# Batched 64x64 matrix products: b three tiles ahead instead of four, half of two a tiles as fp32, and casts and result blocks given to other engines

## The chip, the cores and the metric

The kernel runs on one core of a Trainium2 chip. The metric is the device time of one execution in microseconds (us), the median of several. A profile gives a span, which is about 1.8 us shorter than the time of the same execution. MB are millions of bytes, and a "tile" of b or of the result is 64 matrices (1 MiB as fp32), of a 128 matrices (2 MiB).

## The reference

```python
a: float32 (1024, 64, 64);  b: float32 (1024, 64, 64)
return np.matmul(a, b).astype(np.float32)      # float32 (1024, 64, 64)
```

So 33.55 MB are read and 16.78 MB are written, with little arithmetic for each byte.

## The kernel before

There are 8 tiles of a (index s) and 16 of b and of the result (index t). A tile of a comes in four quarters (h): three are cast to bf16 by the DMA itself, on GpSimd's queue, the fourth comes as fp32 and VectorE casts it (the very first tile comes wholly as fp32). TensorE transposes a, VectorE spreads it into a block-diagonal tile, casts b to bf16, and ScalarE (for odd tiles VectorE too) moves the products from PSUM to SBUF. b comes on SyncE's queue for even t and on ScalarE's for odd t; all results go out on GpSimd's queue.

```python
A_AHEAD = 3;  B_AHEAD = 4                       # buffers of a_pool and of b_pool
...
def load_a(s):
    a_sb = a_pool.tile([128, 3, 16, 64], bf16, name="a_sb")
    for h in range(3):
        nc.gpsimd.dma_start(out=a_sb[:, h, :, :]..., in_=a_v[s, h])
    a_raw = a_pool.tile([128, 16, 64], fp32, name="a_raw")
    nc.sync.dma_start(out=a_raw[:]..., in_=a_v[s, 3])
...
def load_b(t):
    b_sb = b_pool.tile([128, 16, 128], fp32, name="b_sb")
    queue = nc.scalar if t % 2 else nc.sync
    queue.dma_start(out=b_sb[:], in_=b_v[t])
...
for t in range(n_t):                            # s, half = t // 2, t % 2
    if t + 1 < n_t:
        spread(t + 1)
        cast(t + 1)
    if t + B_AHEAD < n_t:
        load_b(t + B_AHEAD)
    if half == 0 and 0 < s < n_s - 1 - A_AHEAD:
        load_a(s + 1 + A_AHEAD)
    if half == 0 and 0 < s < n_s - 1:
        transpose(s + 1, 1)
    multiply(t)
    ...                                         # regroup, transpose(s + 2, 0), store(t - 1)
```

## Time and profile before

| | before |
|---|---|
| time, median of 4 | 135.45 us (135.24 to 135.5) |
| span of the profile | 133.8 us |
| busiest engines | VectorE 71%, ScalarE 66% |
| HBM bytes per time, from 4 us to the last read | 399 GB/s |
| last packet of a read, of a store | 109.65, 131.9 us |

On each queue the packets follow the order of issue, so adding up their sizes tells when each transfer began and ended. A packet of a casting load counts twice, since it reads twice the bytes that it writes. "The end of the reads" below is always the end of the last packet of a or b. Packet times here are counted from the zero of the profile's views; those in the prediction lie 0.25 us later, which changes no difference between two of them, but makes a wait from an issue to a packet look 0.25 us longer.

These are the last stretches of the kernel before: start and end, length, then busy time of PE, PEld, DVE, ACT and POOL with the number of instructions, granted clock, DMA share and GB/s.

```profile
108.00:116.00 8.00, 5.22 (x105) 4.90 (x101) 7.24 (x10) 6.88 (x13) 2.25 (x2) 0.57 1.03 402
116.00:124.00 8.00, 2.04 (x64) 1.92 (x64) 4.72 (x11) 5.22 (x12) 4.52 (x6) 0.89 1.02 372
124.00:134.00 10.00, 0.00 (x0) 0.00 (x0) 0.00 (x0) 0.00 (x0) 0.00 (x0) 0.50 0.67 231
```

In the last 10 us no engine computes at all; the DMA share of 0.67 is that of the last stores. Whatever is computed a few microseconds later than here costs nothing, as long as the stores in front of it are still going out.

### The profile page before, as it was taken

Reading aid. Unit: us, or ns where it says so; the run is one execution under the profiler, and the core shown is the slowest. Engines: PE = TensorE matmul, PEld = TensorE weight load, DVE = VectorE, ACT = ScalarE, POOL = GpSimd, SP = SyncE. Lnnn points to the kernel's source line nnn. Section 1 sums busy time; section 2 is a strip of 40 time slices with the busy share of each in tenths; the row PEclk is TensorE's granted clock in tenths of the full one; section 3 lists DMA queues with packets and bytes.
Section 4 is the critical chain, followed back from the end, with each engine's and each line's share of the span. In section 5 each row is a group of like instructions: output and inputs, shape, how many; then the busy total and the mean of one; then the engine's idle time right before and its main releaser. Section 6 shows DMA issues by size and latency. Waiting matters only on the chain.

```text
span 133.8 us, 2832 instructions
## 1 busy us (share of the span) xinstructions
PE 65.7 (49%) x1152; PEld 62.7 (47%) x1152; DVE 94.6 (71%) x120; ACT 87.7 (66%) x161; POOL 38.5 (29%) x49
## 2 busy tenths in 40 slices
PE   0007307970077463749919744991876376640000
PEld 0007207970077353649909744991866266630000
DVE  5930499108997059999999999899959989992000
ACT  3225424998038996758998985899793987992000
POOL 8991000420091080334124042003301220637000
PEclk9999999999559999555996896589677775797555
DMA  3999999999999999999999999999999999999991
GB/s 75 376 331 311 306 315 311 307 301 309 306 307 382 366 312 309 388 397 397 317 304 352 399 392 377 314 307 364 398 385 391 392 401 398 404 388 353 338 334 42
DMA packets 17485, 45.01 MB, mean 336 GB/s; under 512 B 1088, under 2 KB 1088, under 8 KB 17472
## 3 DMA queue, kind: packets, MB, share of 16 engines
q0 software_dynamic: 7440, 22.28, 54.8%
q1 hardware_dynamic: 5520, 13.11, 27.0%
q10 hardware_dynamic: 4512, 9.44, 18.6%
q8 instruction: 9, 0.15, 0.4%
q14 instruction: 4, 0.03, 0.1%
HBM read 33.55 MB, written 16.78 MB: 376 GB/s over the span
## 4 chain that ended last, share of the span: by engine, by line
DMA 35%; SPq 27%; DVE 15%; issue 6%; ACT 3%; POOL 3%; PE 3%; POOLq 1%; DVEq 0%; ACTq 0%
SPq L72 22%; DMA a_raw<-in_a_dram 18%; DMA b_sb<-in_b_dram 17%; DVE at_bd L128 8%; DVE b_bf L139 5%; SPq L91 3%; POOL out_dram L161 3%; PE o_ps L184 3%; ACT o_sb L172 2%; DVE o_sb L172 1%; SPq L85 1%; ACT b_bf L146 1%; DVE a_bf L106 1%; DVE a_bf L103 1%; POOLq L278 1%
## 5 line engine op out<-in xcount | busy, mean ns | idle before, releaser
L172 ACT COPY o_sb<-o_ps 64x512 f32<-64x512 f32 x106 | 61.6, 581 | 14.3 <-PE o_ps L184 13.0
L184 PEld LDWEIGHTS <-at_bd 128*128 128x128 bf16 x1024 | 41.6, 111 | 34.9 <-DVE b_bf L139 22.4
L184 PE MATMUL o_ps<-b_bf,at_bd 128*128 128x64 bf16 x960 | 41.9, 215 | 31.1 <-DVE b_bf L139 20.9
L128 DVE COPY at_bd<-at_sb 32x1024 f32<-32x1024 f32 x64 | 46.0, 719 | 13.4 <-ACT at_sb L118 11.6
L161 POOL DMA_DIRECT2D out_dram<-o_sb x20 | 20.6, 1031 | 58.1 <-ACT o_sb L172 21.4
L115 PE MATMUL at_ps<-identity,a_bf 128*128 128x128 f32 x128 | 23.4, 360 | 20.6 <-ACT a_bf L100 11.0
L115 PEld LDWEIGHTS at_ps<-identity,a_bf 128*128 128x128 f32 x128 | 21.6, 196 | 20.8 <-issue 19.3
L118 ACT COPY at_sb<-at_ps 128x512 f32<-128x512 f32 x32 | 16.9, 596 | 8.2 <-PE at_ps L115 8.0
L68 POOL DMA_DIRECT2D a_sb<-in_a_dram x21 | 13.9, 673 | 25.9 <-DVE a_bf L103 19.9
L139 DVE CAST b_bf<-b_sb 128x2048 bf16<-128x2048 f32 x14 | 17.4, 1245 | 2.9 <-DMA b_sb<-in_b_dram 2.6
L172 DVE COPY o_sb<-o_ps 64x512 f32<-64x512 f32 x14 | 9.7, 690 | 0.6 <-ACT o_sb L172 0.3
L106 DVE CAST a_bf<-a_raw 128x1024 bf16<-128x1024 f32 x7 | 5.5, 792 | 5.7 <-DMA a_raw<-in_a_dram 5.7
L103 DVE COPY a_bf<-a_sb 128x3072 bf16<-128x3072 bf16 x7 | 7.0, 1006 | 0.0
L100 ACT CAST a_bf<-o_sb 128x1024 bf16<-128x1024 f32 x2 | 2.1, 1044 | 5.0 <-DMA o_sb<-in_a_dram 5.0
L139 ACT CAST b_bf<-b_sb 128x2048 bf16<-128x2048 f32 x1 | 1.9, 1898 | 3.8 <-DMA b_sb<-in_b_dram 3.8
L100 DVE CAST a_bf<-o_sb 128x1024 bf16<-128x1024 f32 x2 | 2.8, 1380 | 1.9 <-DMA o_sb<-in_a_dram 1.9
L212 DVE MEMSET at_bd<- 128x4096 f32 x1 | 3.5, 3472 | 0.8 <-issue 0.8
L172 DVE COPY o_sb<-at_ps 64x256 f32<-64x256 f32 x8 | 3.4, 422 | 0.3 <-PE at_ps L184 0.2
L172 ACT COPY o_sb<-at_ps 64x256 f32<-64x256 f32 x8 | 2.9, 367 | 0.1
L209 ACT ACT_TABLE_LOAD x1 | 1.3, 1283 | 2.3 <-issue 2.3
L184 PE MATMUL at_ps<-b_bf,at_bd 128*128 128x64 bf16 x64 | 2.0, 193 | 1.2 <-DVE at_bd L128 1.2
L217 POOL MEMSET at_bd<- 128x2048 f32 x1 | 1.8, 1849 | 0.0
(12 smaller groups left out, 5.5 us busy)
## 6 DMA issues: line engine op xcount, KB each, us to landing
out_dram<-o_sb POOLq DMA_DIRECT2D x14, 1024.0 KB, 23.6
a_sb<-in_a_dram POOLq DMA_DIRECT2D x21, 256.0 KB, 17.4
a_raw<-in_a_dram SPq DMA_DIRECT2D x7, 512.0 KB, 24.2
o_sb<-in_a_dram ACTq DMA_DIRECT2D x2, 512.0 KB, 7.0
o_sb<-in_a_dram SPq DMA_DIRECT2D x2, 512.0 KB, 5.9
out_dram<-o_sb POOLq DMA_DIRECT2D x2, 512.0 KB, 11.4
out_dram<-o_sb POOLq DMA_DIRECT2D x4, 256.0 KB, 10.1
b_sb<-in_b_dram SPq DMA_DIRECT2D x8, 0.5 KB, 22.2
```

What stands on the lines that cost most here:

```text
L68: nc.gpsimd.dma_start(out=a_sb[:, h, :, :].rearrange("p v k -> p (v k)"), in_=a_v[s, h])
L72: nc.sync.dma_start(out=a_raw[:].rearrange("p v k -> p (v k)"), in_=a_v[s, 3])
L100: copy(a_bf[:, :, h, :], a_sb[h].rearrange("p (v k) -> p v k", v=16))
L103: nc.vector.tensor_copy(a_bf[:, :, 0:3, :], cast_sb[:].rearrange("p h v k -> p v h k"))
L106: nc.vector.tensor_copy(a_bf[:, :, 3, :], raw[:])
L115: nc.tensor.transpose(at_ps[:, vo, :], a_cols[:, 4 * vo + 2 * j + wl, :], identity[:])
L118: nc.scalar.copy(at_tiles[s][:, j, :, wl, :, :], at_ps[:].rearrange("p vo (g mp) -> p g mp vo", mp=4),)
L128: nc.vector.tensor_copy(bd[rows, :, :, :, h, :].rearrange("p j g wl mo -> p j (g wl) mo"), at_tiles[t // 2][rows, :, half, :, :, :].rearrange(
L139: (nc.vector.tensor_copy if t else nc.scalar.copy)(b_bf[:], b_sb[:])
L161: nc.gpsimd.dma_start(out=o_v[t, :, lo : lo + n, :], in_=o_sb[:, lo : lo + n].rearrange("p gh j wl n -> p (gh j wl n)"),)
L172: copies[2 * par + wl](dst, src)
L184: nc.tensor.matmul(o_ps[:, gl, g % 2, j, :], at_bd[:, j, g, :, u], b_bf[:, g, 64 * u : 64 * u + 64], start=(u == 0), stop=(u == 1),)
```

## The change

The intent, as I read it: an earlier end of the tail. GpSimd's queue, which carries all results, gets two casting loads less; VectorE gives two casts of b to GpSimd; ScalarE gives result blocks to VectorE; and a b buffer is given up, which pays for the two new fp32 buffers.

```diff
-    B_AHEAD = 4
+    B_AHEAD = 3
+    x_pool = ctx.enter_context(tc.tile_pool(name="x_pool", bufs=2))
...
     def load_a(s):
+        n_cast = 3 if s < n_s - 2 else 2
         a_sb = a_pool.tile([128, 3, 16, 64], bf16, name="a_sb")
-        for h in range(3):
+        for h in range(n_cast):
             nc.gpsimd.dma_start(...)
-        a_raw = a_pool.tile([128, 16, 64], fp32, name="a_raw")
-        nc.sync.dma_start(..., in_=a_v[s, 3])
+        for h in range(n_cast, 4):
+            pool = a_pool if h == 3 else x_pool
+            raws[h] = pool.tile([128, 16, 64], fp32, name=f"a_raw{h}")
+            queue = nc.sync if h == 3 else nc.scalar
+            queue.dma_start(..., in_=a_v[s, h])
...                                             # regroup: one VectorE cast for each fp32 quarter
     def cast(t):
-            (nc.vector.tensor_copy if t else nc.scalar.copy)(b_bf[:], b_sb[:])
+                engine = nc.gpsimd if t >= n_t - 3 else nc.vector      # t = 0 stays on ScalarE
+                engine.tensor_copy(b_bf[:], b_sb[:])
...
-                if half and t % 2:
+                if half and (t % 2 or t >= n_t - 4):
                     copies[2:] = [nc.vector.tensor_copy] * 2
...
         transpose(0, 1)
-        load_b(3)
         spread(0)
```

More of the change, by code (lines that the diff above doesn't have):

```diff
@@ L70, in load_a @@
             )
-        a_raw = a_pool.tile([128, 16, 64], fp32, name="a_raw")
-        nc.sync.dma_start(out=a_raw[:].rearrange("p v k -> p (v k)"), in_=a_v[s, 3])
-        a_tiles[s] = a_sb, a_raw
+        raws = {}
+        for h in range(n_cast, 4):
+            pool = a_pool if h == 3 else x_pool
+            raws[h] = pool.tile([128, 16, 64], fp32, name=f"a_raw{h}")
+            queue = nc.sync if h == 3 else nc.scalar
+            queue.dma_start(out=raws[h][:].rearrange("p v k -> p (v k)"), in_=a_v[s, h])
+        a_tiles[s] = a_sb, raws
     def load_first_a():
@@ L101, in regroup @@
         else:
-            cast_sb, raw = a_sb
+            cast_sb, raws = a_sb
+            n_cast = 4 - len(raws)
             nc.vector.tensor_copy(
-                a_bf[:, :, 0:3, :], cast_sb[:].rearrange("p h v k -> p v h k")
-            )
-            nc.vector.tensor_copy(a_bf[:, :, 3, :], raw[:])
+                a_bf[:, :, 0:n_cast, :],
+                cast_sb[:, 0:n_cast].rearrange("p h v k -> p v h k"),
+            )
+            for h, raw in raws.items():
+                nc.vector.tensor_copy(a_bf[:, :, h, :], raw[:])
         abf_tiles[s] = a_bf
@@ L138, in cast @@
         if t < n_t - 1:
-            (nc.vector.tensor_copy if t else nc.scalar.copy)(b_bf[:], b_sb[:])
+            if t == 0:
+                nc.scalar.copy(b_bf[:], b_sb[:])
+            else:
+                engine = nc.gpsimd if t >= n_t - 3 else nc.vector
+                engine.tensor_copy(b_bf[:], b_sb[:])
         else:
```

## The prediction

> **What bounds the kernel now.** I read the slices of the page first, then its queues, then the waits of the SyncE queue, then the trace's packet records (start, size and queue of every DMA packet), which I added up per queue in stretches of 4 us.
>
> ```profile
> PE 65.7 (49%) x1152; PEld 62.7 (47%) x1152; DVE 94.6 (71%) x120; ACT 87.7 (66%) x161; POOL 38.5 (29%) x49
> ...
> DMA  3999999999999999999999999999999999999991
> GB/s 75 376 331 311 306 315 311 307 301 309 306 307 382 366 312 309 388 397 397 317 304 352 399 392 377 314 307 364 398 385 391 392 401 398 404 388 353 338 334 42
> ...
> q0 software_dynamic: 7440, 22.28, 54.8%
> q1 hardware_dynamic: 5520, 13.11, 27.0%
> q10 hardware_dynamic: 4512, 9.44, 18.6%
> ...
> HBM read 33.55 MB, written 16.78 MB: 376 GB/s over the span
> ```
>
> No compute engine is above 71%, while the DMA row is full from the second slice to the last but one. The GB/s row seems to dip to 310 wherever a tiles are fetched, but it counts what is written: a casting load of a reads 512 KB and writes 256 KB. Counted by HBM bytes (a cast packet twice), the packet records give 383 to 412 GB/s in every 4 us stretch from 4 to 120 us, 398 in the mean. Only the ends fall short: 0.36 MB in the first 4 us, and 353, 343 and 253 GB/s in the stretches from 120 to 132 us.
>
> ```profile
> SPq L278 <- DMA out_dram<-o_sb: 41.8, 3, 40.8
> ```
>
> ```profile
> 118.34 3.03 ACT L172 COPY o_sb<-at_ps 64x256 f32<-64x256 f32 x8
> 118.61 0.75 POOL L161 DMA_DIRECT2D out_dram<-o_sb  x1 [1.46 <-ACT o_sb L172]
> 120.14 2.96 POOL L161 DMA_DIRECT2D out_dram<-o_sb  x4 [0.77 <-ACT o_sb L172]
> ```
>
> These are the SyncE queue's final wait (for stores) and the end of the timeline. Computing is over at 121.4 us; the last store packet starts near 132 us. Stores go out in order on the GpSimd queue (q0), so its packets tell when each is served: tile 12's store is issued at 108.7 and begins at 118.9, tile 13's at 113.8 and 121.9, tile 14's at 116.2 and 124.9, tile 15's at 120.1 and 127.9. Every late store waits 8 to 10 us behind earlier ones. The kernel is **bound by DMA bytes**; the chain of waits, which names SyncE's a_raw issues and b loads, describes the order in which a full pipe serves them. Its weight there comes from this line of the a_raw tile:
>
> ```profile
> L72 SPq DMA_DIRECT2D a_raw<-in_a_dram x7: 550/11657/13702, 3.3 to 65.5; - x7
> ```
>
> A hardware-queue issue normally takes 0.7 us (b_sb: 707 ns); an a_raw issued right behind a b load holds its sequencer for 6 to 14 us, until roughly a tenth to a quarter of that b tile has moved.
>
> **What the Trainium skill says.** "DMA: Bandwidth & Descriptors", Queues, rings and completion order: each DMA engine goes round its queue rows packet by packet. The trace agrees: while all three queues have work, b moves at about 100 GB/s on q1 and 93 on q10 in 2 KB packets, stores at about 190 on q0 in 4 KB packets. Same page, Specifications: 358 GB/s of HBM per core and a fabric ceiling of 435; this case measures 398, between them, and I use 398. "GPSIMD Engine Reference", Performance versus the Vector engine: 1.03 cycles per element for the shortest loop bodies and 1.8 for the best longer one, at 1.2 GHz, so I estimate a 2048-element cast at 1.8 to 3.1 us. The trace has no GpSimd cast; its 2048-element memset took 1.85 us. "SBUF — State Buffer", SBUF: two separate sides: GpSimd and a VectorE operation in a two-port mode lock each other out for a whole instruction. No GpSimd compute meets VectorE late in this trace, so no run yet shows it.
>
> **The change part by part.**
>
> *b three ahead.* The same 16 loads; from tile 3 on each is allowed one tile later. The b casts are (110.38 - 51.70)/10 = 5.9 us apart (tiles 4 to 14). On ScalarE's queue b landed early: last packet to cast is 14.5, 9.8, 6.5, 6.4 and 8.0 us for tiles 5, 7, 9, 11, 13, so 5.9 us later mostly fits. On SyncE's queue b lands just in time (3 us or less from tile 8 on), but there it waits for the queue and not for its buffer: tile 12 is issued at 77.6 and starts at 88.8, tile 14 at 88.2 and 98.5. A 5.9 us later issue is absorbed. In the start-up, b tile 3 is issued after ScalarE's cast of tile 0 (ends 20.97) instead of at 14.77; its queue then idles from 19.65 to about 22.5 and the other two take the bandwidth. It also puts a_raw 3 ahead of b 4 on SyncE's queue, which should remove the 5.7 us for which VectorE waited for a_raw at 42.5; b 4 itself then lands near the time at which it was cast before (51.7), so I count no gain. **Sum 0.**
>
> *Half of the last two a tiles as fp32.* Two 512 KB reads move from q0 to q10. HBM bytes are unchanged (50.33 MB). Cast stretches run near 402 GB/s and cast-free ones near 394: 1.05 MB costs 0.05 us more. GpSimd saves two issues of 0.67 us; VectorE's 3072-element bf16 copy (0.955 us) becomes 2048 elements plus one more 1024-element cast (0.69), some 0.4 us more on each of two tiles, off the DMA path. The new load is issued from ScalarE right behind a b load, so the hold seen on SyncE can occur on an engine that computes: I estimate 1.5 to 4 us of held ScalarE at tiles 4 and 6, when the results of those tiles wait for it. **Sum +0.1 on the DMA, up to 8 us of ScalarE that the pipe should hide.**
>
> *GpSimd casts tiles 13 and 14.* VectorE loses 2 x 1.23 us, GpSimd gains 2 x (1.8 to 3.1) us and VectorE may be locked out for as long. The stores of tiles 11 and 12 stand behind these casts in GpSimd's order, so they are issued some 3 to 5 us later; they had 13 and 10 us to spare. **Sum 0.**
>
> *VectorE takes two result blocks from tile 12 on.* For tiles 12 and 14, two copies each: ScalarE loses 4 x 0.58 = 2.3 us, VectorE gains 4 x 0.69 = 2.8 us. The last computing may end a microsecond earlier, but tile 15's store waits 7.8 us for its turn anyway. **Sum 0.**
>
> So the sum is 135.4 + 0.05 to 0.1. The best case: the first 4 us as they are, the other 49.97 MB at 398 GB/s (125.6 us), 1.6 us from the last packet to the end of the span (132.2 to 133.8), and 1.65 us by which the time exceeds the span: 4 + 125.6 + 1.6 + 1.65 = 132.9 us, 1.9% down. **That is the ceiling of any gain**, and nothing in the change speaks to the slow last 12 us directly.
>
> **The rivals.** First, *ScalarE becomes a bound*: two holds of up to 4 us delay evacuation, hence PE, hence later stores. For it: ScalarE shows 9, so 90% or more, in many of the later slices, and holds of 12 us are there on SyncE. Against it: q10's previous b tile should be nearly through, and the late stores have 8 us to spare. If the holds are 10 us each, the backlog is used up and the time becomes 137 to 140. Second, *starvation*: with three b buffers the reads could end later and the stores be served sooner, so that the final backlog shrinks and the tail computing (b 15 landed to last store issued, some 10 us) comes into the open. For it: q10 will idle for some microseconds early on. Against it: loading and computing step every 5.9 us, while a tile's whole DMA (a, b and out, 3.15 MB) takes 7.9 us at 398 GB/s, so the stores fall behind by the difference. It would cost 1 to 4 us. Third, *a quicker tail*: if the slow last 12 us come from one queue writing alone, moving 1 MB off q0 shortens them; 3.8 MB at 340 rather than 398 costs 1.6 us in all, so a gain of 0.3 to 1 us, 134.5.
>
> **Range and chances.** The sum says 135.4, the third rival pulls down by up to 1, the other two up by more but with little weight. I predict **135.2 us, range 133.7 to 137.4**. Faster by over 2% needs less than 132.7, below the ceiling of 132.9: 0.03. Slower by over 2% needs the first two rivals to eat 8 us of backlog and 2.7 more: 0.07. Within 2%: 0.90.
>
> **What would show it.** Right: the DMA row full as before, the same 398 GB/s of HBM bytes in the middle, computing over 5 us or more before the last packet, the a_raw wait at 42 us gone, casts of 2 to 4 us on GpSimd. Wrong: a DMA slice under 9 in the middle or late, late stores served at once after issue, or a ScalarE issue of an fp32 a load lasting over 8 us. A rate above 400 GB/s would also break it.

## The result, and the profile after

The changed kernel takes 136.27 us (median of 4, 136.11 to 136.49) against 135.45: a ratio of 1.0064, 95% interval 1.0044 to 1.0085. Here and below a ratio is the mean time of one kernel's fast runs over the mean of the other's in the same rounds, so not quite the ratio of the medians. It is 0.6% slower: inside the stated range and "within 2%", but clear of noise, and on the other side of the stated centre.

The page of the changed kernel: slices and queues, to be held against those of before in the prediction.

```profile
DMA  3999999999999999999999999999999999999693
GB/s 78 365 331 310 307 314 278 277 308 328 328 324 392 304 327 347 389 394 388 317 349 393 403 389 335 326 396 386 395 394 393 392 394 394 390 381 350 232 319 110
...
q0 software_dynamic: 7152, 21.76, 52.5%
q1 hardware_dynamic: 5520, 13.11, 26.7%
q10 hardware_dynamic: 4800, 10.49, 20.4%
```

The bytes moved as told: 1.05 MB more on q10 (ScalarE), the 0.52 MB that two casting loads write off q0. The middle is nearly as full as before (397 GB/s of HBM bytes from 4 us to the last read, against 399). What is new is the 6 in the third slice from the end, with 232 GB/s: the DMA engines wait there. The stretches of the end say for what.

```profile
116.00:124.00 8.00, 6.29 (x128) 6.12 (x127) 5.14 (x8) 4.99 (x10) 3.90 (x4) 0.56 1.00 373
124.00:134.00 10.00, 0.11 (x4) 0.00 (x0) 4.76 (x10) 3.23 (x9) 3.78 (x6) 0.62 0.72 244
```

From 124 us on, VectorE still works for 4.8 us and ScalarE for 3.2, where both were done before. The issues of the last stores, from the timeline of the changed kernel:

```profile
117.02 0.89 POOL L175 DMA_DIRECT2D out_dram<-o_sb  x1
...
119.34 1.40 POOL L175 DMA_DIRECT2D out_dram<-o_sb  x1 [1.42 <-issue]
...
123.41 0.77 POOL L175 DMA_DIRECT2D out_dram<-o_sb  x1 [2.67 <-ACT o_sb L186]
...
126.27 2.94 POOL L175 DMA_DIRECT2D out_dram<-o_sb  x4 [2.10 <-ACT o_sb L186]
129.54 0.72 POOL L175 DMA_DIRECT2D out_dram<-o_sb  x1 [0.33 <-DVE o_sb L186]
```

By the packet records tile 12's store starts at 119.1, tile 13's at 122.0, tile 14's at 125.1: 2.1, 2.7 and 1.7 us after their issue, where they stood in line for 10.0, 7.8 and 8.4 us before. At tile 14's second half the line is gone: it is issued at 126.27 and starts at 127.6, and from 126 to 128 us the DMA moves 221 and then 137 GB/s. Computing ends at 129.25 us (before: 121.4), the last packet at 132.9.

The reason is upstream: the reads end at 118.9 us, 9.3 us later than before. From there the chain is serial: b tile 15's casts at 119.58, its products from 121.28, its blocks copied out until 129.25. The total of the reads is the same, and nearly the rate; the stores were only served earlier and the reads later. The change's own blocks stand in this chain too: VectorE ends last, 1.9 us after ScalarE (127.4), because it first copies two blocks of tile 14 (1.39 us from 124.33).

ScalarE's holds are there too. These are its issues of the new fp32 loads:

```profile
52.20 5.15 ACTq L79 DMA_DIRECT2D a_raw<-in_a_dram  x1
...
66.89 4.68 ACTq L79 DMA_DIRECT2D a_raw<-in_a_dram  x1
```

So there were three suspects: reads that end late because fewer b loads are in flight (theory 1 below), the holds of ScalarE (theory 2, a part of theory A), and a tail in which GpSimd's casts or VectorE's blocks take longer (theories 3 and B).

### The profile page after: what moved, and what is told of

The parts are those of the page before. It is cut to its first block, busy times and chain, and to the rows that moved or that the text cites. A ratio compares the mean times of both kernels' runs of the same rounds, so it can differ in the third digit from the quotient of the medians.

```text
span 134.7 us, 2843 instructions
## 1 busy us (share of the span) xinstructions
PE 64.7 (48%) x1152; PEld 62.1 (46%) x1152; DVE 94.2 (70%) x124; ACT 85.5 (63%) x157; POOL 41.3 (31%) x49
## 4 chain that ended last, share of the span: by engine, by line
ACT 25%; DMA 23%; PE 18%; DVE 14%; issue 7%; ACTq 5%; POOL 2%; SPq 1%; POOLq 1%
DMA b_sb<-in_b_dram 23%; ACT o_sb L186 19%; PE o_ps L198 12%; DVE at_bd L138 7%; PE at_ps L125 6%; DVE o_sb L186 4%; ACT at_sb L128 4%; ACTq L79 4%; DVE b_bf L153 2%; POOL out_dram L175 2%; ACT b_bf L150 1%; ACTq L98 1%; SPq L92 1%; DVE a_bf L111 1%; POOLq L291 1%
## 5 line engine op out<-in xcount | busy, mean ns | idle before, releaser
L186 ACT COPY o_sb<-o_ps 64x512 f32<-64x512 f32 x102 | 59.3, 581 | 8.5 <-PE o_ps L198 7.1
L198 PEld LDWEIGHTS <-at_bd 128*128 128x128 bf16 x1024 | 43.2, 113 | 42.8 <-DVE b_bf L153 16.3
L125 PE MATMUL at_ps<-identity,a_bf 128*128 128x128 f32 x128 | 21.3, 337 | 19.1 <-ACT a_bf L107 11.4
L125 PEld LDWEIGHTS at_ps<-identity,a_bf 128*128 128x128 f32 x128 | 19.5, 181 | 19.1 <-issue 19.1
L153 DVE CAST b_bf<-b_sb 128x2048 bf16<-128x2048 f32 x12 | 15.1, 1260 | 8.2 <-DMA b_sb<-in_b_dram 8.0
L71 POOL DMA_DIRECT2D a_sb<-in_a_dram x19 | 12.2, 655 | 21.6 <-DVE a_bf L111 19.5
L186 DVE COPY o_sb<-o_ps 64x512 f32<-64x512 f32 x18 | 12.4, 690 | 8.9 <-ACT o_sb L186 8.6
L153 POOL CAST b_bf<-b_sb 128x2048 bf16<-128x2048 f32 x2 | 4.1, 2066 | 10.9 <-DMA b_sb<-in_b_dram 10.9
L111 DVE COPY a_bf<-a_sb 128x3072 bf16<-128x3072 bf16 (+1 forms) x7 | 6.1, 877 | 0.0
L160 ACT CAST b_bf<-b_sb 128x512 bf16<-128x512 f32 x2 | 1.1, 615 | 2.9 <-DMA b_sb<-in_b_dram 2.9
```

What stands on the lines that cost most here:

```text
L71: nc.gpsimd.dma_start(out=a_sb[:, h, :, :].rearrange("p v k -> p (v k)"), in_=a_v[s, h])
L111: nc.vector.tensor_copy(a_bf[:, :, 0:n_cast, :], cast_sb[:, 0:n_cast].rearrange("p h v k -> p v h k"),)
L125: nc.tensor.transpose(at_ps[:, vo, :], a_cols[:, 4 * vo + 2 * j + wl, :], identity[:])
L153: engine.tensor_copy(b_bf[:], b_sb[:])
L186: copies[2 * par + wl](dst, src)
L198: nc.tensor.matmul(o_ps[:, gl, g % 2, j, :], at_bd[:, j, g, :, u], b_bf[:, g, 64 * u : 64 * u + 64], start=(u == 0), stop=(u == 1),)
```

## The experiments

All twelve were timed in five rounds against the kernel before, and all gave correct results.

### Each part alone

**e1_b3**, three b buffers and tile 3's load moved, nothing else:

```diff
-    B_AHEAD = 4
+    B_AHEAD = 3
...
-        load_b(3)
```

> The kernel before with three b buffers, nothing else. Theory 1 (fewer b loads in flight end the reads late, the stores catch up, and the last computing is no longer hidden by a backlog of stores): the last b packet moves from 110 us to 115 us or later, computing ends less than 6 us before the last packet, time +0.4 to +1.0 us (135.8 to 136.5). Theory 2 (the holds of ScalarE behind its fp32 a loads cause it): within 0.3 us of before, reads end near 110.

Measured: 135.03 us, ratio 0.9964 (0.9948 to 0.998). Faster, which neither theory had said. Yet the reads do end late, at 116.0 us, as theory 1 held. The loss that it drew from them did not come: computing ends 6.0 us before the last packet, and tile 14's first store still waits 3.8 us for its turn.

**e2_half**, the fp32 quarters alone, with four b buffers:

```diff
+        n_cast = 3 if s < n_s - 2 else 2
+            queue = nc.sync if h == 3 else nc.scalar      # and the rest of load_a and regroup
```

> The kernel before with half of the last two a tiles as fp32, issued from ScalarE, b still four ahead. Theory 1: time within 0.3 us of before, although ScalarE shows two issues of 3 to 6 us; reads end by 113. Theory 2: the two holds delay the evacuations, reads end at 115 or later, time +0.5 us or more.

Measured: 134.71 us, ratio 0.9943 (0.9928 to 0.9958), the reads end at 112.55 us. Faster again, which again neither theory had said. And there is no hold: both issues on ScalarE take 0.57 us. With four buffers an even step loads an even b tile, on SyncE; with three it loads an odd one, on ScalarE, right in front of the fp32 quarter. The hold comes from a parity that the change moved.

**e3_pool** and **e4_dve**, the casts and the blocks alone:

```diff
+                engine = nc.gpsimd if t >= n_t - 3 else nc.vector       # e3_pool
```
```diff
+                if half and (t % 2 or t >= n_t - 4):                    # e4_dve
```

> The kernel before with GpSimd casting b tiles 13 and 14. Theory 1: the stores of tiles 11 and 12 are issued 3 to 6 us later and still wait their turn; time within 0.3 us. Theory 3 (the casts stand before stores in GpSimd's order and the tail pays for them): +0.5 us or more, with late stores served as soon as they are issued.

> The kernel before with VectorE taking two result blocks from tile 12 on. All theories: within 0.2 us, since the last stores wait 8 us in any case; if the tail computing were on the path of the kernel before, 0.5 to 1 us faster.

Measured: 135.53 us, ratio 1.0002 (0.9989 to 1.0015), and 135.73 us, ratio 1.0014 (0.9998 to 1.003). Both are nothing, with reads ending at 110.3 and 110.4 us: behind 8 us of waiting stores the tail's computing is free, as predicted.

What follows: the parts are not additive in time (two of them gain, two do nothing, together they lose), but they are additive in the end of the reads. e1 moves it by 6.3 us, e2 by 2.9, together 9.2; the change moves it by 9.3. This suggests that time first falls and then rises as the reads end later.

### Parts undone

**e5_after_b4**, the changed kernel with four b buffers:

```diff
-    B_AHEAD = 3
+    B_AHEAD = 4
...
+        load_b(3)
```

> The changed kernel with four b buffers again, all else kept. Theory A (the holds of ScalarE come from an fp32 a load issued in the same step as an odd b load, which only three buffers put there; with later reads they expose the tail): the two ScalarE issues fall from 5 us to 0.6, last b packet at 112 to 114, computing ends 5 us or more before the last packet, time 134.4 to 135.0. Theory B (the GpSimd casts or VectorE's blocks lose the 0.8 us): stays at 135.8 or more.

Measured: 134.58 us, ratio 0.9939 (0.9925 to 0.9953), reads end at 112.8 us, both issues 0.57 us. Its DMA row is full to the end:

```profile
DMA  3999999999999999999999999999999999999992
GB/s 72 376 332 311 306 313 315 308 301 304 308 307 376 374 314 309 378 392 408 371 308 361 418 394 382 312 348 398 392 393 391 392 394 395 404 401 384 355 337 99
```

Theory B falls as the sole cause: GpSimd's casts and VectorE's blocks are all in this kernel. Going from four b buffers to three turns 0.9939 into 1.0064, though by itself it gained 0.4%. What VectorE's blocks cost once the tail is in the open was not tested: no run takes them out of the changed kernel.

**e7_after_swap**, the same bytes on the same queue without the hold:

```diff
+            if half == 0 and 0 < s < n_s - 1 - A_AHEAD:
+                load_a(s + 1 + A_AHEAD)
             if t + B_AHEAD < n_t:
                 load_b(t + B_AHEAD)
-            if half == 0 and 0 < s < n_s - 1 - A_AHEAD:
-                load_a(s + 1 + A_AHEAD)
```

> The changed kernel with load_a ahead of load_b in each step, so that ScalarE issues the fp32 a load first and the b load behind it: the same bytes on the same queue without the hold. If the hold is what delays: both issues under 1 us, b tile 15's last packet at 117.5 or earlier, time 134.8 to 135.5. If the 1 MB more on ScalarE's queue is what delays: last packet at 118.5 or later, time 136.0 or more.

Measured: 136.18 us, ratio 1.0049 (1.0033 to 1.0065), reads end at 118.3 us, and the holds are gone:

```profile
48.81 0.57 ACTq L79 DMA_DIRECT2D a_raw<-in_a_dram  x1
51.28 0.69 ACTq L98 DMA_DIRECT2D b_sb<-in_b_dram  x1
61.58 0.57 ACTq L79 DMA_DIRECT2D a_raw<-in_a_dram  x1
65.60 0.69 ACTq L98 DMA_DIRECT2D b_sb<-in_b_dram  x1
```

So 9 us less of held ScalarE gains nothing that the intervals can tell from zero. The holds, which looked like the culprit in the trace, are not the cause: without them the reads end almost as late.

**e8_after_nopool**, VectorE casting b tiles 13 and 14 again:

```diff
-                engine = nc.gpsimd if t >= n_t - 3 else nc.vector
-                engine.tensor_copy(b_bf[:], b_sb[:])
+                nc.vector.tensor_copy(b_bf[:], b_sb[:])
```

> The changed kernel with VectorE casting b tiles 13 and 14. GpSimd's casts take 2.2 and 1.9 us against 1.23 on VectorE. Theory A: in an exposed tail these 1.7 us count, but reads still end at 118 or later and both holds stay: 135.4 to 136.2. Theory B: back to 135.4 or less with late stores waiting again.

Measured: 136.23 us, ratio 1.0067 (1.0042 to 1.0092), reads end at 118.3 us. No different from the changed kernel; GpSimd's casts are neither gain nor loss.

**e6_after_sp**, both fp32 quarters on SyncE's queue:

```diff
-            queue = nc.sync if h == 3 else nc.scalar
-            queue.dma_start(...)
+            nc.sync.dma_start(...)
```

> The changed kernel with the second fp32 a load on SyncE's queue instead of ScalarE's. Theory A: no held ScalarE, reads end at 115 to 117.5 instead of 119, time 134.6 to 135.4. Theory B: 135.8 or more.

Measured: 139.19 us, ratio 1.0273 (1.0245 to 1.0301): a clear miss. ScalarE is not held and the reads end 1 us sooner (117.9 us), but b tiles 13 and 14 end at 110.4 and 116.1 us, against 108.1 and 114.4 in the changed kernel, and the stores of tiles 12 and 13 are issued at 119.2 and 122.5, 2.2 and 3.2 us later. So the last b tile alone does not tell the end; those before it can be late too. How much of the 3 us comes from this was not separated.

### The end of the reads

**f1_late4** was meant to load tiles 12 to 15 one step earlier, with a buffer of its own for tile 12:

```diff
...                                             # b12_pool, one buffer, for tile 12
-            if t + B_AHEAD < n_t:
-                load_b(t + B_AHEAD)
+            for n in {8: (11, 12), 9: (13,), 10: (14,), 11: (15,)}.get(t, (t + 3,)):
+                if n < n_t:
+                    load_b(n)
```

> The changed kernel with one buffer more for b tile 12, so that tiles 12 to 15 are loaded one step earlier while everything up to tile 11 stays three ahead. If the late b loads at the end are what exposes the tail (the lateness arises at the end): the last b packet comes at 113 to 116, no DMA slice under 9 before the last two, time 134.4 to 135.3. If the lateness is built up from the start (tile 3 late, queues idle early): last packet at 118 or later and time 135.8 or more.

Measured: 144.83 us, ratio 1.0688 (1.0668 to 1.0709). The edit was wrong: at t = 12 the default loads tile 15 a second time, and that issue made ScalarE wait. The result is correct, the run says nothing of the theory, but it shows how dear a wait in front of a DMA issue is on an engine that computes:

```profile
116.48 0.02 ACT L100 MOVE_SHAPE b_sb<-in_b_dram  x1 [11.38 <-DMA b_sb<-in_b_dram]
```

**f4_late4** is the same without the second load (the default becomes `(t + 3,) if t < 8 else ()`):

> The run f1 as it was meant (f1 loads b tile 15 twice by a mistake of the edit): the changed kernel with one buffer more for b tile 12, so that tiles 12 to 15 are loaded one step earlier. In the changed kernel ScalarE's queue is busy without a break from 55.8 to 95.9 us and then idles 1.6 and 1.2 us between b 11, 13 and 15. If only the last loads matter, these 2.8 us go: last b packet at 116 to 117, time 135.0 to 135.6. If the lateness is built up early (tile 3 issued late, 1 MB more on the queue) and the queue stays behind: last packet at 118 or later, time 135.8 to 136.3.

Measured: 135.43 us, ratio 0.999 (0.9966 to 1.0014), reads end at 116.2 us, as the first outcome said. Taking 2.7 us from the end of the reads, with the rest of the change kept, takes 0.7% from the time. With e5 this shows the link from late reads to the loss. Its remaining distance to e1 (0.9964 at nearly the same end of reads) has a visible candidate, VectorE beside GpSimd's cast; tile 14's copies before, then here:

```profile
107.00 3.09 DVE L128 COPY at_bd<-at_sb 32x1024 f32<-32x1024 f32 x4
...
112.54 1.89 POOL L155 CAST b_bf<-b_sb 128x2048 bf16<-128x2048 f32 x1 [0.94 <-DMA b_sb<-in_b_dram]
112.57 4.83 DVE L140 COPY at_bd<-at_sb 32x1024 f32<-32x1024 f32 x4
```

The four copies take 1.7 us more, about the length of the cast. VectorE's blocks, which e1 lacks, are another candidate. What makes the 0.25% was not tested.

**f3_half3**, e5 with three half-fp32 tiles instead of two:

```diff
-        n_cast = 3 if s < n_s - 2 else 2
+        n_cast = 3 if s < n_s - 3 else 2
```

> The changed kernel with four b buffers and the last three a tiles half fp32. If a later end of the reads is what gains, as long as the tail stays hidden: last b packet at 114 to 115.5, time 134.2 to 134.6, no worse than with two. If the gain came from something else in the fp32 loads themselves (fewer casting loads): 0.3 us faster, with the reads ending where they did.

Measured: 137.27 us, ratio 1.0128 (1.01 to 1.0156), reads end at 115.4 us. The end of the reads is as expected, the time is a miss. The edit left two buffers for what were now three fp32 quarters, so the third load waits, on ScalarE, for VectorE to free one; its next copy stood for 7.6 us:

```profile
73.56 1.07 ACT L128 COPY at_sb<-at_ps 128x512 f32<-128x512 f32 x2 [7.64 <-DVE a_bf L116]
```

The run therefore doesn't tell how far a later end of reads gains. It does tell that the end of reads is not the only thing that must be in time.

**f2_hwtail**, e5 with the stores of tiles 14 and 15 on SyncE's queue:

```diff
-            nc.gpsimd.dma_start(
+            queue = nc.gpsimd if t < n_t - 2 else nc.sync
+            queue.dma_start(
                 out=o_v[t, :, lo : lo + n, :],
```

> The changed kernel with four b buffers (the best so far), with the stores of tiles 14 and 15 on SyncE's queue instead of GpSimd's. If the low rate of the last 10 us (about 350 GB/s) belongs to one software queue writing alone: the rate there returns to 390 or more and the time falls to 133.6 to 134.2. If it belongs to writing alone, whatever the queue: 134.3 to 134.9.

Measured: 134.53 us, ratio 0.9932 (0.992 to 0.9944), against 0.9939 for e5: no difference. In the stretch from 124 to 128 us, now served by the hardware queue, the rate is 353 GB/s (e5: 350). So the low rate at the end is no property of GpSimd's queue.

### The table

| run | reads end, us | from there to the last packet: us, GB/s | GB/s in its first 8 us, last 4 us | ratio to before |
|---|---|---|---|---|
| before | 109.65 | 22.3, 350 | 401, 248 | 1 |
| e3_pool | 110.26 | 21.7, 350 | 400, 256 | 1.0002 |
| e4_dve | 110.44 | 21.3, 352 | 401, 270 | 1.0014 |
| f2_hwtail | 112.35 | 18.7, 357 | 399, 270 | 0.9932 |
| e2_half | 112.55 | 18.4, 358 | 401, 280 | 0.9943 |
| e5_after_b4 | 112.78 | 18.0, 360 | 396, 297 | 0.9939 |
| e1_b3 | 115.98 | 15.6, 345 | 398, 221 | 0.9964 |
| f4_late4 | 116.17 | 15.9, 333 | 360, 302 | 0.9990 |
| e8_after_nopool | 118.33 | 13.9, 317 | 356, 292 | 1.0067 |
| e7_after_swap | 118.33 | 13.9, 322 | 349, 301 | 1.0049 |
| after | 118.91 | 14.0, 306 | 339, 289 | 1.0064 |

Left out are e6 and f3, whose middle tiles were late too, and f1. Two things work against each other.

The gain is measured, its mechanism is open. It is not that stores alone are slower than stores mixed with reads: in the kernel before and in e1, e2, e3, e4, e5 and f2 they move 396 to 401 GB/s for 8 us after the last read, as much as the mix. This is e1, whose reads end at 116.0:

```profile
116.00:124.00 8.00, 4.74 (x86) 4.42 (x83) 6.11 (x13) 7.16 (x14) 2.34 (x3) 0.62 1.03 402
```

At 118 us the kernel before and e5 have the same bytes left, 4.48 and 4.46 MB, so the later reads have gained nothing until then. All of the 1.1 us by which e5's last packet comes sooner arises afterwards: the rate stays near 400 GB/s for longer (it falls from 118.7 us before, with tile 12's store, from some 120 us in e5 and from 126 in e1), and the last 4 us are less slow (297 GB/s against 248). No run shows why the rate falls, nor why later with later reads.

The loss is the tail's chain. The last b tile needs some 14 us until its last store is out: the three runs with the latest reads all have a tail of 13.9 or 14.0 us. In them the tail is that chain, its mean rate sinks to 306 to 322 GB/s because the stores are no longer there in time, and the gain is gone. The best version is e5, or f2, its equal: 134.5 us, faster than both kernels by 0.6 and 1.2%.

## Why the prediction was right or wrong

The number was within the range and in the class with a chance of 0.90; the centre, 135.2, was 1.1 us too low, on the wrong side of before. That the error is so small is in part luck: a gain and a loss, both weighed only as rivals, nearly cancel.

- **The bound** was right. The DMA moved 396 to 399 GB/s from 4 us to the last read in all valid runs, whatever the change. The ceiling of 132.9 us was not touched by any run.
- **"5.9 us later mostly fits", "Sum 0"** is the step that failed. I asked of each b tile whether it would still meet its own cast, and left out what its queue does meanwhile. I did name the idle start of ScalarE's queue, from 19.65 to about 22.5 us, but mis-sized it: b tile 3 is issued at 21.7 in the changed kernel, and its first packet comes 4.2 us later, at 25.9. (The trace of before had such a delay on an empty queue: b tile 7, issued at 43.7, starts at 47.8.) In e1 this queue stands empty from 19.8 to 25.4 us and from 37.3 to 43.3; before, those transfers followed one another within 0.7 us. Over the whole run its gaps sum to 17.7 us in e1, against 10.4 before. While the two other queues have work, this one gets about 95 GB/s, and its last load ends 6.3 us later. That "the other two take the bandwidth" was true, and not enough: what the pipe is full of decides what is left for the end.
- **Half of the last two a tiles, "Sum +0.1 on the DMA"** was right in bytes and wrong in its effect: these loads moved the reads' end by another 2.9 us, and alone they gained 0.6%. That is the size of my third rival, 0.3 to 1 us (e2 measured 0.7), but not its reason: the slow end is not "one queue writing alone", since one queue alone moved 401 GB/s for 8 us in the kernel before, and SyncE's queue in its place at the end did not help (f2). The size was luck.
- **The holds of ScalarE** were there, 5.15 and 4.68 us against an estimate of 1.5 to 4. That the pipe hides them was right: e7 took them away and gained nothing clear.
- **The 8 us by which stores wait in line** were taken for a reserve that the change leaves alone. It ate all but some 2 us of them. The second rival (reads later, stores sooner, the tail in the open) is what happened, at a net 0.8 us, because the third rival's gain stands against it. e5 to after, where only its own part changes, is 1.7 us.
- **GpSimd's casts: 0** was right (2.24 and 1.90 us, e3, e8), though the stores behind them came 8 us later rather than 3 to 5, mostly because b itself came late. The lock between GpSimd and VectorE that the prediction took from "SBUF — State Buffer", SBUF: two separate sides, fits what later runs show: a VectorE cast of 1.23 us took 2.80 us beside a GpSimd cast in f3, and four copies 4.83 instead of 3.09 in f4.
- **VectorE's blocks: 0, perhaps a microsecond earlier.** The 0 was right, the microsecond was not: VectorE's two blocks start when ScalarE's six have ended, so nothing runs side by side; in the changed kernel's open tail they may even cost something, which no run tests. Of the waits, first the kernel before, then the changed one (total us, times, longest):

```profile
DVE o_sb L172 <- ACT o_sb L172: 0.3, 1, 0.3
```

```profile
DVE o_sb L186 <- ACT o_sb L186: 8.6, 5, 2.3
```

- **The signs that I named:** the a_raw wait at 42 us is gone, as said (4.04 us of wait for b tile 4 stand in its place at 46 us). A slice under 9 late, and late stores served at once, were named as signs of being wrong; both are there, and computing ends 3.6 us before the last packet instead of 5 or more.

## What to carry to other kernels

In a kernel bound by DMA bytes, a full DMA row is not the end of the question: ask which transfers are left when the last input arrives, and whether they last longer than the chain from that input to its store. Fewer buffers or more bytes on one queue can move the end of that queue's loads (here by 6.3 and 2.9 us), even where each load still meets its own deadline; add such shifts up before combining changes, because two that gain alone can lose together. And before a mean rate is taken for a cause, look at its course: 350 GB/s in the tail of the kernel before was 401 at first and 248 at last.

## What the Trainium skill lacked or had wrong

- "DMA: Bandwidth & Descriptors", Issuing engines are not separate DMA queues, calls the sequencer's time to start a DMA "usually small relative to the DMA itself". Here an issue on a hardware queue right behind a 1 MiB load in 512-byte runs held SyncE for 3.6 to 13.7 us (before and after) and ScalarE, which computes, for 4.7 and 5.2; it took 0.57 us on ScalarE where the load in front had been moving for at least 1.6 us (e2, e5, e7).
- "DMA: Bandwidth & Descriptors", Specifications, gives about 358 GB/s as the HBM limit of a core, as the prediction cites, and does not say there what its section Bandwidth says: that this is the share with both cores of a pair streaming. One core alone moved 399 GB/s of HBM bytes for over 100 us in mixed reads and writes.
- No page that I read has the fall in the rate of stores at the end: before, from 401 GB/s in the first 8 us after the last read to 248 in the last 4, with GpSimd's queue alone; in f2, with the last two tiles on SyncE's queue, from 399 to 270.
